# A two-layer hybrid block on one core: the experts' later tokens fetched by indirect DMA, their outputs added from a table in DRAM

## The chip, the core and the metric

The kernel runs on one core of a Trainium2 chip. A core has five engines with a queue of instructions each: TensorE (PE in the profile; its weight loads are PEld) multiplies matrices into PSUM banks, VectorE (DVE) and ScalarE (ACT) work on tiles in SBUF and PSUM, GpSimd (POOL) and SyncE (SP) here issue transfers, which 16 DMA engines carry out. Engines wait for each other by semaphores. The metric is the time of one execution on the device in microseconds; lower is better.

## What is computed

The input is 256 latent tokens and 256 context tokens of width 1024, all in float32, batch 1. An even layer (spatial gating beside windowed attention, then a dense SwiGLU) is followed by an odd layer (a recurrent block, then a mixture of experts) and a final RMSNorm. The change lies in the experts:

```python
def swiglu(t, w1, w3, w2):
    return (jax.nn.silu(t @ w1) * (t @ w3)) @ w2

def moe_swiglu(h, router_w, w1, w3, w2):
    logits = (t @ router_w).astype(jnp.float32)
    top_v, top_i = lax.top_k(logits, TOP_K)              # 2 of 8 experts
    gk = jax.nn.softmax(top_v, axis=-1)
    gates = jnp.sum(jax.nn.one_hot(top_i, N_EXPERTS) * gk[..., None], axis=1)
    for e in range(N_EXPERTS):
        out = out + gates[:, e:e + 1] * swiglu(t, w1[e], w3[e], w2[e])

    x = x + g2 * moe_swiglu(rmsnorm(x, n2) * (1.0 + sc2) + sh2, router_w, w1, w3, w2)
```

Per expert w1 and w3 are 1024 x 2816 and w2 is 2816 x 1024, so the eight experts' weights are 277 MB. Each token uses two experts, 64 tokens per expert on average.

## The kernel before

**Three products for one.** A float32 product is formed as three TensorE products of two-part numbers (`mm3`, L335 to L338): each operand is a high part, rounded to TensorE's 32-bit format, and a low part, the rest. So every half of a weight tile (128 x 1024 numbers, half of a raw tile of 1 MB) is split: ScalarE casts the high part `wh` (L126), VectorE subtracts it to get the low part `wl` (L127).

**The weight stream.** The class `Stream` has the list of all weight tiles in the order of their use (`units`). `pump_dma` issues a tile's load on the SP queue (L112) as soon as a raw buffer is free; there are twelve of them in the expert stage. `pump` issues the splits as soon as a pair of split buffers is free; there are five pairs (`HA`, `HB`). `get` hands a half to the matmuls, and what was put off with `later(n, f)` is issued n calls of `get` later.

**Experts.** Up to 128 tokens per expert are gathered into 128 slots. A dispatch matrix of zeros and ones (`make_disp`, `put_disp`, L1325) has a row per token and a column per slot. For a pair of experts `gather` multiplies the normalised rows (high and low part, `h2H`, `h2L`, tile hH) by the pair's 256 columns, 32 matmuls of 256 columns (L1381); this gives the rows already turned, features in partitions. ScalarE applies scale and shift (L1399) and casts (L1404), VectorE subtracts (L1405), into `xTH` and `xTL` (tile hLa).

An expert's 2816 inner columns are worked in six steps (`steps`, widths `GW`, five of 512 and one of 256). In each, `moe_p` forms t @ w1 and t @ w3 in one PSUM bank each (tag mm, four banks); ScalarE applies Silu (L1432), VectorE multiplies (L1434) into `s1`; `moe_t` turns it with TensorE transposes (L1441), and ScalarE and VectorE split it into `mg` (L1448, L1451); `moe_o` multiplies by w2 into two banks per expert (tag po). The loop over k issues `moe_p` of step k, then `moe_o` of step k-1, then `moe_t` of step k. Weight rows of w1 and w3 are 2 KB in a tile of four blocks of 128 rows (1 KB in the last step), those of w2 4 KB.

After an expert's last step `moe_y` multiplies the output by the layer's gate (L1485) and splits it (L1486, L1487). `combine` brings it back to tokens: the dispatch matrix, turned (`turn_disp`, L1414), times the output, 4 x 2 matmuls of 512 columns (L1495, L1496), and VectorE adds each of the four results, times the router's gate, to the residual `Xl` (L1498). Should an expert have over 128 tokens, `overflow` repeats it for the rest at the end.

**Order.** The functions are called in the order of the program, but a scheduler places each instruction on its engine's queue by its own reckoning of when its inputs are there; `issue_after` forces an order between two. Within a queue the order is fixed.

Of the kernel before, what the change touches and what calls it, by code (L numbers as in the profile page):

```python
# [14 lines left out]
I32 = mybir.dt.int32  # L15
# [196 lines left out]
def tile_block(ctx, tc, a, out):  # L212
# [3 lines left out]
    GW = [512] * 5 + [256]  # L216
# [37 lines left out]
    def moe_p_units(e, g, w1, w3):  # L254
        r = []
        for nm, w in (("m1", w1), ("m3", w3)):
            if GW[g] == 512:
                r += [kunit((nm, e, g, u), w, 4 * u, 4, 512 * g, 512) for u in range(2)]
            else:
                r.append(kunit((nm, e, g, 0), w, 0, 8, 512 * g, 256))  # L260
        return r

    def moe_o_units(e, g, w2):
        return [kunit(("m2", e, g, u), w2, 4 * g + 2 * u, 2, 0, D) for u in range(GW[g] // 256)]
# [32 lines left out]
    steps = [(e, g) for e in range(NE) for g in range(6)]  # L297
# [9 lines left out]
    NRAW, NRAW_X, NRAW_B = 4, 1, 7 - 1  # L307
# [366 lines left out]
    with ExitStack():  # L674
# [643 lines left out]
        yt, mg, n_t = [], [], [0]  # L1318
# [16 lines left out]
        def route_rest():  # L1335

            d = moe.tile([P, 4, 2], F32, name="dr")
            V.tensor_tensor(d[:, 0], mx[:, :, 1], mx[:, :, 0], op=ALU.subtract)
# [29 lines left out]
        xT, yo, gTs, yHL, dTs = {}, {}, {}, {}, {}  # L1368

        def gather(dst_key, dsp, n):  # L1370

            tH = moe.tile([P, KT, 256], F32R, tag="xTH", name=nm("xTH"))
            tL = xTL
            done = []
            terms = [(h2H, 0), (h2L, 0), (h2H, 1), (h2L, 1)]

            def add(p, c2, x):
                h, i = terms[x]
                for j in range(2):
                    cs = slice(P * (2 * c2 + j), P * (2 * c2 + j) + P)  # L1380
                    T.matmul(p[:, 256 * j:256 * j + n], h[:, i, cs], dsp(i), start=(x == 0 and j == 0), stop=(x == 3 and j == 1))  # L1381
            if dst_key == 0:
                ps = [mm() if c2 < 2 else po() for c2 in range(KT // 2)]
                for x in range(3):
                    for c2 in range(KT // 2):
                        add(ps[c2], c2, x)
            for c2 in range(KT // 2):
                if dst_key == 0:
                    p = ps[c2]
                    add(p, c2, 3)  # L1390
                else:
                    p = tr()
                    for x in range(4):
                        add(p, c2, x)
                js = slice(2 * c2, 2 * c2 + 2)
                tm = ht().rearrange("p (j f) -> p j f", j=2)[:, :, :n]
                for j in range(2):
                    c = 2 * c2 + j
                    x = S.activation(tm[:, j], p[:, 256 * j:256 * j + n], AF.Identity,  # L1399
                                     scale=AB[:, 1, 0, 0, c:c + 1], bias=AB[:, 1, 0, 1, c:c + 1])  # L1400
                if dst_key == 0:
                    V.tensor_copy(tH[:, js, :n], tm)  # L1402
                else:
                    S.copy(tH[:, js, :n], tm)  # L1404
                y = V.tensor_tensor(tL[:, js, :n], tm, tH[:, js, :n].bitcast(F32), op=ALU.subtract)  # L1405
                done.append((x, y))
            xT[dst_key] = tH, tL
            return done
# [9 lines left out]
        def moe_p(s_, e, g, x, c0):  # L1418
            xh, xl = x
            w = GW[g]  # L1420
            p1, p3 = mm(), mm()
            nk = 1024 // w
            s1 = ht()
            for name, p in (("m1", p1), ("m3", p3)):
                for u in range(8 // nk):
                    wH, wL = views(s_.get((name, e, g, u // 2)), nk)
                    for k in range(nk):
# [231 lines left out]
```

## Time and profile before

| | us |
|---|---|
| median of three runs (1600.59 to 1602.11) | 1601.19 |
| the profiled execution's own time | 1600.52 |
| its span, first to last instruction | 1598.7 |
| TensorE busy | 1551.5 |
| VectorE busy | 1286.8 |
| ScalarE busy | 981.1 |
| GpSimd busy | 0.2 |

The expert stage runs from about 808 us, where its first matmul starts, to 1582 us. What follows is the last expert's combine, the final norm and the stores. Busy time says how much an engine had to do, not whether the others waited for it: that is read from the waits and from the chain of work that ended last. TensorE's matmuls overlap in the records, so the cost of one on the path is the distance between the starts of two.

### The profile page before, as it was taken

How to read it: one execution, taken by the hardware profiler on the slowest of the kernel's cores; microseconds unless marked ns; L12 is line 12 of the kernel's file. 1: busy time of each engine (PE TensorE's matmuls, PEld its weight loads, DVE VectorE, ACT ScalarE, POOL GpSimd, SP SyncE). 2: the span in 40 equal slices, each digit the busy share in tenths (PEclk: the TensorE clock that was granted, in tenths of full speed). 3: DMA queues.
4: the chain of work that ended last, by engine and by line, in shares of the span. 5: the costliest groups of instructions: out<-in, count | busy, mean ns of one | idle time of the engine just before them, and what ended most of it. 6: DMA issues, size and time to landing. Idle time of an engine off the chain costs nothing.

```text
span 1598.7 us, 20230 instructions
## 1 busy us (share of the span) xinstructions
PE 1551.5 (97%) x7518; PEld 1237.4 (77%) x7518; DVE 1286.8 (80%) x1817; ACT 981.1 (61%) x1292; POOL 0.2 (0%) x4
## 2 busy tenths in 40 slices
PE   5999999999999999999999999999999999999996
PEld 3775787888888887776578888888888888888885
DVE  3577557475877576599899998998989899898987
ACT  4435625322222224679688877887778777877775
POOL 0000000000000000000000000000000000000000
PEclk9999999999999999999999999999999999999998
DMA  8867143444536441414699989999999999999980
GB/s 296 284 220 241 49 134 106 158 134 156 193 124 211 156 142 57 132 53 164 213 358 352 378 325 370 322 380 354 363 363 330 369 364 367 336 346 367 365 303 29
DMA packets 204267, 398.22 MB, mean 249 GB/s; under 512 B 7930, under 2 KB 66552, under 8 KB 204160
## 3 DMA queue, kind: packets, MB, share of 16 engines
q1 hardware_dynamic: 201184, 395.34, 69.7%
q10 hardware_dynamic: 2976, 1.50, 0.4%
q8 instruction: 61, 1.00, 0.3%
q14 instruction: 46, 0.38, 0.1%
HBM read 395.76 MB, written 1.05 MB: 248 GB/s over the span
## 4 chain that ended last, share of the span: by engine, by line
PE 87%; DVE 8%; ACT 2%; DMA 2%; issue 1%; ACTq 0%; DVEq 0%
PE mm L337 18%; PE mm L336 18%; PE mm L338 18%; PE po L337 8%; PE po L338 8%; PE po L336 8%; PE po L430 1%; PE tr L1441 1%; DVE wl L127 1%; PE po L983 1%; PE tr L1381 1%; PE tr L968 1%; DVE xn L500 1%; DMA raw<-in_w_in_e_dram 1%; DMA raw<-in_ada_w_o_dram 1%
## 5 line engine op out<-in xcount | busy, mean ns | idle before, releaser
L126 ACT CAST wh<-raw 128x1024 fp32r<-128x1024 f32 (+1 forms) x644 | 662.5, 1046 | 447.0 <-PE mm L337 145.4
L127 DVE TENSOR_TENSOR wl<-raw,wh 128x1024 fp32r<-128x1024 f32 (+1 forms) x644 | 759.4, 1214 | 127.5 <-ACT wh L126 115.9
L338 PE MATMUL mm<-wh,hLa 128*128 128x512 f32 (+1 forms) x800 | 299.2, 374 | 0.1
L337 PE MATMUL mm<-wl,xTH 128*128 128x512 f32 (+1 forms) x768 | 289.9, 377 | 0.0
L336 PE MATMUL mm<-wh,xTH 128*128 128x512 f32 (+1 forms) x768 | 287.3, 374 | 0.9 <-DVE xTH L1402 0.9
L336 PE MATMUL mm<-hH,wh 128*128 128x512 f32 (+1 forms) x608 | 228.7, 378 | 1.7 <-ACT gT L1148 1.5
L338 PE MATMUL mm<-hH,wl 128*128 128x512 f32 (+1 forms) x608 | 224.8, 371 | 0.5 <-DVE wl L127 0.5
L338 PEld LDWEIGHTS mm<-wh,hLa 128*128 128x128 f32 x800 | 150.9, 189 | 26.4 <-DVE hLa L1405 1.3
L337 PEld LDWEIGHTS mm<-wl,xTH 128*128 128x128 f32 x768 | 144.8, 189 | 27.1 <-DVE wl L127 3.0
L336 PEld LDWEIGHTS mm<-wh,xTH 128*128 128x128 f32 x768 | 144.8, 188 | 26.5 <-DVE xTH L1402 1.5
L337 PE MATMUL po<-wl,mg 128*128 128x512 f32 x352 | 137.4, 390 | 0.0
L338 PE MATMUL po<-wh,mg 128*128 128x512 f32 x352 | 136.4, 390 | 0.0
L336 PEld LDWEIGHTS mm<-hH,wh 128*128 128x128 f32 x608 | 114.2, 189 | 24.0 <-issue 2.0
L338 PEld LDWEIGHTS mm<-hH,wl 128*128 128x128 f32 x608 | 114.5, 188 | 20.1 <-DVE wl L127 0.7
L336 PE MATMUL po<-wh,mg 128*128 128x512 f32 x352 | 128.9, 391 | 0.0
L337 PE MATMUL mm<-hLb,wh 128*128 128x512 f32 (+1 forms) x304 | 112.9, 372 | 0.6 <-DVE hLb L616 0.6
L337 PE MATMUL mm<-hLa,wh 128*128 128x512 f32 (+1 forms) x304 | 112.8, 371 | 0.5 <-DVE hLa L616 0.5
L500 DVE SCALAR_TENSOR_TENSOR xn<-raw,act,xn 128x512 f32<-128x512 f32 x112 | 81.7, 747 | 1.2
L337 PEld LDWEIGHTS po<-wl,mg 128*128 128x128 f32 x352 | 66.2, 188 | 13.8 <-DVE wl L127 0.4
L336 PEld LDWEIGHTS po<-wh,mg 128*128 128x128 f32 x352 | 66.2, 188 | 13.5
L338 PEld LDWEIGHTS po<-wh,mg 128*128 128x128 f32 x352 | 66.0, 188 | 13.5
L337 PE MATMUL po<-wl,gH 128*128 128x512 f32 x176 | 69.9, 397 | 0.0
(392 smaller groups left out, 1873.9 us busy)
## 6 DMA issues: line engine op xcount, KB each, us to landing
raw<-in_moe_w_dram SPq DMA_DIRECT2D x264, 1024.0 KB
raw<-in_ffn_w_dram SPq DMA_DIRECT2D x33, 1024.0 KB
raw<-in_ada_w_e_dram SPq DMA_DIRECT2D x24, 1024.0 KB
raw<-in_ada_w_o_dram SPq DMA_DIRECT2D x24, 1024.0 KB
raw<-in_w_in_o_dram SPq DMA_DIRECT2D x10, 1024.0 KB
raw<-in_w_in_e_dram SPq DMA_DIRECT2D x7, 1024.0 KB
raw<-in_w_out_o_dram SPq DMA_DIRECT2D x5, 1024.0 KB
raw<-in_w_out_e_dram SPq DMA_DIRECT2D x2, 1024.0 KB
```

The costliest lines, as they stand in the source:

```text
L126: sp = (self.nc.scalar.copy(hv, src), self.nc.vector.tensor_tensor(lv, src, hv.bitcast(F32), op=ALU.subtract))
L127: self.nc.vector.tensor_tensor(lv, src, hv.bitcast(F32), op=ALU.subtract))
L336: T.matmul(dst, aH, bH, start=start, stop=False)
L337: T.matmul(dst, aH, bL, start=False, stop=False)
L338: return T.matmul(dst, aL, bH, start=False, stop=stop)
L430: T.matmul(p[32 * g:32 * g + 32, :], act[:, 4 * u + g, :], w[:, g, :], start=(u == 0), stop=(u == 1))
L500: V.scalar_tensor_tensor(acc[s_], w[:, k, :], c, acc[s_], op0=ALU.mult, op1=ALU.add)
L968: T.transpose(p[:, P * b:P * b + P], pr[:, P * b:P * b + P], ident)
L983: T.matmul(ob[c][0][64 * i:64 * i + 64, P * t:P * t + P], vv[:, b, 64 * i:64 * i + 64], pts[i][:, P * jj:P * jj + P], start=(jj == 0), sto ...
L1381: T.matmul(p[:, 256 * j:256 * j + n], h[:, i, cs], dsp(i), start=(x == 0 and j == 0), stop=(x == 3 and j == 1))
L1441: T.transpose(p[:, P * j:P * j + P], s1[:, P * j:P * j + P], ident)
```

## The change

**Weights.** The inner columns are worked in three steps of 1024, 1024 and 768. A raw tile of w1 or w3 has two blocks of 128 rows with 4 KB (3 KB in the last step) per row; a half is one block. `moe_p` now fills two banks for w1 and then two for w3; `s1` is a tile of its own of 1024 columns with one buffer (tag s1), and `mg` has one buffer instead of two halves. The raw buffers in the stage are eleven instead of twelve.

**Later tokens.** Only the first pair is gathered by matmuls (`gather_first`). GpSimd forms the normalised rows (`tokens`, in two halves, in the buffer with tag s1) and stores them in a table `Hd` in DRAM. `places` computes, for each token and choice, the slot (`put`) and the row of the output table (`take`); four indirect DMAs write the token's number into the slot's place in `Td`, which is read back as `slots`. `rows_of` fetches a later pair's rows from `Hd` by these numbers, during the even expert before, and `turn_slots` turns them with 16 transposes; scale, shift and split follow as before (`modulated`).

**Outputs.** `moe_y` of experts 0 to 6 stores the gated output in a table `Yd`; neither the split nor `combine` is done for them. `combine_table` fetches for each token and choice the row of `Yd` (a row of zeros where the choice is expert 7 or the token is in the overflow), and `add_table` adds it, times the router's weight, to the residual. Expert 7 goes the old way.

The diff, cut to its core:

```diff
-    GW = [512] * 5 + [256]
+    GW = [1024, 1024, 768]
+    NG = len(GW)
...
     def moe_p_units(e, g, w1, w3):
...
+        return [kunit((nm, e, g, u), w, 2 * u, 2, 1024 * g, GW[g], cut)
+                for nm, w in (("m1", w1), ("m3", w3)) for u in range(KT // 2)]
...
-    NRAW, NRAW_X, NRAW_B = 4, 1, 7 - 1
+    NRAW, NRAW_X, NRAW_B = 4, 1, 5
...
+        def rows_of(idx):
+
+            r = big("hH", [P, len(idx), D], F32)
+            for x, ids in enumerate(idx):
+                nc.gpsimd.indirect_dma_start(r[:, x, :], None, Hd[:, :], bass.IndirectOffsetOnAxis(ap=ids, axis=0))
+            return r
+
+        def turn_slots(keys, r):
+
+            tH = x_tile()
+            for c2 in range(KT // 2):
+                p = tr()
                 for j in range(2):
...
+                    for x in range(len(keys)):
+                        c = P * (2 * c2 + j)
+                        T.transpose(p[:, 256 * j + P * x:256 * j + P * x + P], r[:, x, c:c + P], ident)
+                modulated(tH, c2, p, P * len(keys), S.copy)
...
         def moe_p(s_, e, g, x, c0):
+
             xh, xl = x
...
+            cols = [slice(c, min(c + 512, GW[g])) for c in range(0, GW[g], 512)]
+            s1 = moe.tile([P, D], F32, tag="s1", name=nm("s1"))
+            for name in ("m1", "m3"):
+                ps = [mm() for _ in cols]
+                for k in range(KT):
+                    wH, wL = s_.get((name, e, g, k // 2))
+                    for p, cs in zip(ps, cols):
+                        mm3(p[:, :cs.stop - cs.start], xh[:, k, c0:c0 + P], xl[:, k, c0:c0 + P], wH[:, cs], wL[:, cs],
+                            k == 0, k == KT - 1)
...
         def moe_y(e):
...
+            if e in range(NE - 1):
+                y = big("hLb", [P, D], F32)
+                for h in range(2):
+                    cs = slice(512 * h, 512 * h + 512)
+                    V.tensor_tensor(y[:, cs], yo[e][h], gates["ao", 5, 0][:, cs], op=ALU.mult)
+                nc.gpsimd.dma_start(Yd[P * e:P * e + P, :], y)
+                return
...
+        def places():
...
+            for c in range(2):
+                for i in range(2):
+                    nc.gpsimd.indirect_dma_start(Td[:, :], bass.IndirectOffsetOnAxis(ap=put[:, c, i:i + 1], axis=0),
+                                                 toki[:, i:i + 1], None, bounds_check=NE * P - 1, oob_is_err=False)
+            nc.gpsimd.dma_start(slots_of, Td.rearrange("(e p) o -> p (e o)", p=P))
...
+        def add_table(r):
+            for c in range(2):
+                for i in range(2):
+                    V.scalar_tensor_tensor(Xl[:, i, :], r[:, 2 * c + i, :], g12[0][:, 2 + c, i:i + 1], Xl[:, i, :],
+                                           op0=ALU.mult, op1=ALU.add)
...
+        def tokens():
+
+            nc.gpsimd.memset(zero, 0)
+            nc.gpsimd.dma_start(Td.rearrange("(e p) o -> p (e o)", p=P), zero)
...
+            z = moe.tile([P, D], F32, tag="s1", name="zrow")
+            nc.gpsimd.memset(z[0:1, :], 0.0)
+            nc.gpsimd.dma_start(Yd[(NE - 1) * P:, :], z[0:1, :])
+            for t in range(2):
+                r = moe.tile([P, D], F32, tag="s1", name=nm("hrow"))
+                nc.gpsimd.tensor_scalar(r, Xl[:, t, :], rr[t], None, op0=ALU.mult)
+                nc.gpsimd.dma_start(Hd[P * t:P * t + P, :], r)
...
-        done = gather_pair(0)
+        done = gather_first()
+        tokens()
...
+                if e % 2 == 0 and g == 2 and e + 2 < NE:
+                    table[:] = [rows_of([slots_of[:, x:x + 1] for x in (e + 2, e + 3)])]
+                if e % 2 == 1 and g == NG - 1 and e + 1 < NE:
+                    turn_slots((e + 1, e + 2), table.pop())
+            if k >= 2 and steps[k - 2] == (NE - 1, NG - 1):
+                combine(NE - 1, dTs.pop(NE - 1), lambda i: G[:, i, NE - 1:NE])
...
-            if k == 3:
+            if k == 1:
                 with tc.issue_after(st.last[0].ins), tc.issue_after(st.last[1].ins):
                     route_rest()
+                    places()
...
+                if steps[k - 1] == (NE - 2, NG - 1):
+                    table[:] = [combine_table()]
+                if steps[k - 1] == (NE - 1, 0):
+                    with tc.issue_after(st.last[1].ins):
+                        add_table(table.pop())
```

**On GpSimd**, which had nothing of this before, there now stands at the start of the expert stage (with the semaphores that a row waits for; the row ISA in between reloads the engine's library):

```order
L1582 MEMSET zero_6343 128x8 [waits DVE_49,PE_49,Activation_49]
L1589 MEMSET zrow_6491 1x1024
L1583 DMA Td_6342<-zero_6343 128x8x1 [waits Pool_49]
L1590 DMA Yd_6341<-zrow_6491 16x1x64 [waits Pool_49]
L1593 ISA
L1593 TENSOR_SCALAR hrow_808_6494<-Xl_73,n1r_790_6363 128x1024 [waits DMASW1_49,DVE_49]
L1594 DMA Hd_6340<-hrow_808_6494 128x1024 [waits Pool_49]
L1593 TENSOR_SCALAR hrow_809_6497<-Xl_73,n1r_796_6395 128x1024 [waits DMASW2_49,DVE_49]
L1594 DMA Hd_6340<-hrow_809_6497 128x1024 [waits Pool_49]
```

The zero row, the two table rows and the first product tile share one buffer, so each row waits for the store of the one before it. What waits for the last of these stores (DMASW3) is ScalarE's first Silu of the experts, here in ScalarE's queue of the changed kernel among the weight casts:

```order
L126 CAST wh1171_6589<-raw117_6324 128x1024 [waits DVE_49,PE_49]
L126 CAST wh1180_6601<-raw118_6326 128x1024 [waits DMAHW5_49,DVE_49,PE_49]
L1453 ACT_TABLE_LOAD [waits DMASW2_49,DMASW3_49,DMASW1_49]
L1453 ACTIVATE s1_810_6514<-mm_811_6515 128x512 [waits Pool_49]
L126 CAST wh1181_6612<-raw118_6326 128x1024 [waits DVE_49,PE_49]
```

Before, the first Silu waited for its matmuls alone. wh1120 is the first half tile of the experts, so wh1180 is the thirteenth; the first product needs the first eight.

**On TensorE**, at the turn from experts 0 and 1 to 2 and 3, there stood before the gather of the next pair (tr) among the matmuls of the step before (po):

```order
L1381 MATMUL tr_8149<-disp_8019,hH_6338 128x256 x8
L1381 MATMUL tr_8163<-disp_8019,hH_6338 128x256 x8
L336 MATMUL po_7580<-wh_8077,mg 128x512
L1381 MATMUL tr_8177<-disp_8019,hH_6338 128x256 x8
L337 MATMUL po_7580<-wl_8078,mg 128x512
```

and now there stand the transposes of the fetched rows:

```order
L1425 MATMUL tr_8108<-ident,hH_7261 128x128 x4
L1425 MATMUL tr_8118<-ident,hH_7261 128x128 x4
L335 MATMUL po_7818<-wh_8063,mg 128x512
L336 MATMUL po_7818<-wl_8064,mg 128x512
L337 MATMUL po_7818<-wh_8063,mg 128x512
L335 MATMUL po_7819<-wh_8063,mg 128x512
L336 MATMUL po_7819<-wl_8064,mg 128x512
L1425 MATMUL tr_8128<-ident,hH_7261 128x128 x4
```

The 32 gather matmuls of the pair have become 16 transposes, the last four of them four matmuls further down.

**On VectorE**, at the handover into the experts, between the first weight split and the last part of x, the dispatch rows for expert 7 (and its neighbour) have moved up; now there stands:

```order
L127 TENSOR_TENSOR wl_6423<-raw_6176,wh_6422 128x1024
L1324 TENSOR_SCALAR disp_12162<-CT,pos,M 128x128 x2
L1382 CAST xTH_6428<-ht_6459 128x512
L1324 TENSOR_SCALAR disp_12162<-CT,pos,M 128x128
L1383 TENSOR_TENSOR hLa_6337<-ht_6459,xTH_6428 128x512
L1382 CAST xTH_6428<-ht_6466 128x512
L1324 TENSOR_SCALAR disp_12162<-CT,pos,M 128x128
```

Before, the same places followed each other without the rows of L1324 (there L1325). At the end, in the third step of expert 7, the four additions from the table stand in one block:

```order
L127 TENSOR_TENSOR wl3781_13101<-raw378_12845,wh3781_13100 128x768
L1570 SCALAR_TENSOR_TENSOR Xl_73<-hH_1015_12813,dr_6889,Xl_73 128x1024 x4
L127 TENSOR_TENSOR wl3790_13130<-raw379_12871,wh3790_13129 128x768
L127 TENSOR_TENSOR wl3791_13140<-raw379_12871,wh3791_13139 128x768
L1479 TENSOR_TENSOR mg_6693<-tr_1027_13116,mg_6693 128x512
```

Before, four additions of half rows followed each expert's combine.

## Rows read from the trace of the kernel before

**Rows 1.** Page, the span and part 1: busy us, share of the span, instructions

```profile
span 1598.7 us, 20230 instructions
...
PE 1551.5 (97%) x7518; PEld 1237.4 (77%) x7518; DVE 1286.8 (80%) x1817; ACT 981.1 (61%) x1292; POOL 0.2 (0%) x4
```

**Rows 2.** Stretch: its us, each engine's busy us, clock, DMA share, GB/s

```profile
820.00:1560.00 740.00, 740.00 (x3545) 617.83 (x3545) 688.12 (x746) 587.87 (x659) 0.00 (x0) 1.00 0.97 352
```

**Rows 3.** Waits, 820 to 1580 us: total us, times, longest

```profile
ACT wh L126 <- PE mm L338: 65.1, 165, 0.9
...
ACT wh L126 <- DMA raw<-in_moe_w_dram: 7.0, 21, 0.8
```

**Rows 4.** Waits of the SP queue, 820 to 1560 us

```profile
SPq L112 <- DVE wl L127: 565.6, 228, 5.5
```

**Rows 5.** Chain of waits, 850 to 1582 us: shares; start, us, what

```profile
by line: PE mm L337 20.7%; PE mm L336 20.5%; PE mm L338 20.5%; PE po L338 10.7%; PE po L337 10.7%; PE po L336 10.7%; PE tr L1441 2.5%; PE tr L1381 1.6%; PE tr L1496 0.9%; PE tr L1495 0.9%; PE tr L1414 0.2%; PE po L1349 0.0%
...
990.52 1.92 PE tr L1381 x16
```

**Rows 6.** Chain of waits, 1573 to 1600 us

```profile
1573.10 0.12 PE mm L338
...
1574.51 0.46 PE po L338 x2
...
1577.69 0.22 PE tr L1441 x2
```

**Rows 7.** Groups of instructions, 850 to 1582 us, shapes apart

```profile
L1381 PE MATMUL tr<-disp,hH 128*128 128x256 f32 x96 | 13.4, 285 | 0.0
...
L1495 PE MATMUL tr<-hLb,dispT 128*128 128x512 f32 x28 | 11.0, 393 | 0.0
...
L1414 PE MATMUL tr<-ident,disp 128*128 128x128 f32 x16 | 3.1, 273 | 0.0
...
L1498 DVE SCALAR_TENSOR_TENSOR Xl<-tr,G,Xl 128x512 f32<-128x512 f32 x28 | 20.4, 745 | 0.8 <-PE tr L1496 0.8
...
L1487 DVE TENSOR_TENSOR hLb<-ht,hLb 128x512 fp32r<-128x512 f32 x14 | 9.5, 684 | 0.0
L1486 ACT CAST hLb<-ht 128x512 fp32r<-128x512 f32 x15 | 9.1, 620 | 6.0 <-DVE ht L1485 5.6
...
L1399 ACT ACTIVATE ht<-tr,AB 128x256 f32<-128x256 f32 x24 | 12.3, 563 | 4.4 <-PE tr L1381 2.7 <-DVE hLa L1405 1.7
```

**Rows 8.** VectorE in order of time, 786 to 850 us: start, us

```profile
795.98 0.69 DVE L660 TENSOR_TENSOR Xl<-Xl,rtmp 128x512 f32<-128x512 f32 x1
...
801.73 0.60 DVE L1325 TENSOR_SCALAR disp<-CT,pos,M 128x128 fp32r<-128x128 f32 x2
...
803.20 1.28 DVE L1531 SCALAR_TENSOR_TENSOR hH<-Xl,n1r,hH 128x1024 fp32r<-128x1024 f32 x1
...
808.11 0.43 DVE L1402 CAST xTH<-ht 128x512 fp32r<-128x512 f32 x1 [0.58 <-ACT ht L1399]
...
814.51 9.29 DVE L127 TENSOR_TENSOR wl<-raw,wh 128x1024 fp32r<-128x1024 f32 x8
```

**Rows 9.** DMA, 820 to 1560 us: packets, issues of weight tiles

```profile
DMA packets 117547, 260.65 MB, mean 352 GB/s; under 512 B 3984, under 2 KB 20368, under 8 KB 117498
...
raw<-in_moe_w_dram SPq DMA_DIRECT2D x246, 1024.0 KB
```

**Rows 10.** Two stretches of 3 us: 2 KB rows, then 4 KB

```profile
874.00:877.00 3.00, 3.00 (x15) 2.48 (x14) 3.00 (x4) 2.74 (x4) 0.00 (x0) 1.00 1.06 408
1205.50:1208.50 3.00, 3.00 (x15) 2.47 (x14) 3.00 (x4) 2.63 (x4) 0.00 (x0) 1.00 1.01 416
```

**Rows 11.** ScalarE in order of time, 786 to 850 us

```profile
799.39 2.19 ACT L1517 ACTIVATE hH<-Xl,n1r 128x1024 fp32r<-128x1024 f32 x2 [0.15 <-DVE n1r L542]
...
808.86 1.05 ACT L126 CAST wh<-raw 128x1024 fp32r<-128x1024 f32 x1
```

**Rows 12.** VectorE in order of time, 1578 to 1600 us

```profile
1590.15 1.42 DVE L1630 SCALAR_TENSOR_TENSOR xn<-Xl,n1r,fn 128x512 f32<-128x512 f32 x2
```

More of the change, by code (lines that the diff above doesn't have):

```diff
@@ L296, in tile_block @@
     n_dense = len(units)
-    steps = [(e, g) for e in range(NE) for g in range(6)]
+    steps = [(e, g) for e in range(NE) for g in range(NG)]
     for k in range(len(steps) + 1):
@@ L1407, in gather @@
-            xT[dst_key] = tH, tL
-            return done
+                    T.matmul(p[:, 256 * j:256 * j + 256], h[:, i, cs], d[:, i, :], start=(x == 0 and j == 0),
+                             stop=(x == 3 and j == 1))
+            ps = [mm() if c2 < 2 else po() for c2 in range(KT // 2)]
+            for x in range(3):
+                for c2 in range(KT // 2):
+                    add(ps[c2], c2, x)
+            done = []
+            for c2 in range(KT // 2):
+                add(ps[c2], c2, 3)
+                done.append(modulated(tH, c2, ps[c2], 256, V.tensor_copy))
@@ new lines, in moe_t, with evac @@
+            for c in range(0, GW[g], 512):
+                w = min(512, GW[g] - c)
+                p = tr()
+                for j in range(w // P):
+                    T.transpose(p[:, P * j:P * j + P], s1[:, c + P * j:c + P * j + P], ident)
+                def evac(p=p, cs=slice(c, c + w), w=w):
+                    with tc.issue_after(S.copy(gH[:, cs], p[:, :w]).ins):
+                        if last and cs.stop == GW[g]:
+                            S.activation(small.tile([P, 1], F32, tag="warm", name="warm2"), CT[:, C_ONE:C_ONE + 1],
+                                         AF.Sqrt)
+                    V.tensor_tensor(gL[:, cs], p[:, :w], gH[:, cs].bitcast(F32), op=ALU.subtract)
+                if last:
+                    evac()
+                else:
+                    s_.later(2 + c // 512, evac)
@@ L1465, in prod @@
                 return mm3(yo[e][h], gH[:, js], gL[:, js], w[0][:, cs], w[1][:, cs],
-                           g == 0 and k == 0, g == 5 and k == 1)
-            if key == steps[-1]:
-                w = s_.get(("m2", e, g, 0), n=2)
-                for h in range(2):
-                    for k in range(2):
-                        last = prod(k, h, w[k])
-                return last
-            for k in range(GW[g] // P):
+                           g == 0 and k == 0, g == NG - 1 and k == n - 1)
+            end = 2 if key == steps[-1] else 0
+            for k in range(n - end):
                 w = s_.get(("m2", e, g, k // 2))
```

189 lines of the change are left out of this document (97 added, 92 removed).

## The prediction

> **What bounds the kernel now.** I read the page first: the TensorE row is busy for 97% of the span, VectorE for 80%, ScalarE for 61%, GpSimd for nothing (four memsets) [rows 1]. Busy shares are averages over stages, so next came the table of stretches: from 820 to 1560 us, the expert stage, TensorE has no idle time at all, VectorE is at 93% (688 of 740), ScalarE at 79%, the granted clock is 1.00 (the 2.4 GHz level) and the DMA engines have work for 97% of the time [rows 2]. Three engines near their ends: the waits tell which one leads. ScalarE's splitting casts wait for TensorE to give back a split buffer (65.1 us in the first matrices alone), but only 7.0 us in all, in 21 waits of at most 0.8 us, for a weight tile to land [rows 3]. The SP queue, which loads the weights, stood 565.6 of these 740 us waiting for VectorE to finish a raw tile, that is for space [rows 4]. So the weights run ahead, limited by buffers, the splits run ahead, limited by buffers, and what gives buffers back is TensorE. The chain of waits agrees: between 850 and 1582 us all of it is matmuls [rows 5]. A microsecond of TensorE work taken from this stage should be a microsecond of the time, as long as the second (VectorE) and third (DMA) do not become the first.
>
> What one piece costs on that path is read from the distances in the chain, not from the mean durations (0.39 us, which overlap): a 512-column matmul is 0.23 us (two in 0.46), a 256-column one 0.12, a 128x128 transpose 0.11 (two in 0.22) [rows 6].
>
> **The change part by part, on TensorE.** Removed: the gathers of the later three pairs of experts, 3 x 32 = 96 matmuls of 256 columns [rows 7], 16 of them in 1.92 us [rows 5], so 0.12 each and 11.5 us (the chain's 1.6% of 732 us is 11.7). The combine matmuls of experts 0 to 6, 28 of L1495 [rows 7] and as many of L1496, of 512 columns: 56 x 0.23 = 12.9 us (the chain: 1.8% of 732, 13.2). The transposes of the dispatch matrix of seven experts, 14 of the 16 [rows 7]: 14 x 0.11 = 1.5 us. Together 25.9 us. Added: 16 transposes for each of three pairs, 48 x 0.11 = 5.3 us. The sum on TensorE is -20.6 us. The weights' matmuls keep their number and shapes: per expert 48 of 256 columns and the rest of 512, only in another order, and the 22 transposes of the product per expert stay.
>
> **VectorE and ScalarE**, the cover of all this, get lighter. VectorE loses 28 additions into the residual (20.4 us) and 14 subtractions of L1487 (9.5), gains four whole-row additions; the row of that kind and size took 1.28 us (L1531 [rows 8]), so 5.1. ScalarE loses 14 of the 15 casts of L1486 (9.1 us) [rows 7]. The splits grow from 66 to 70 per expert, 16 of them of 768 columns. A full one takes 1.16 us back to back (eight in 9.29 [rows 8]); one of 768 lies between three quarters of that, 0.87, and the whole, and I take 0.9. TensorE uses it up in 3 x 0.23 + 3 x 0.12 = 1.05 us. So VectorE stays the follower in the third group of an expert too, and I cost the new shapes at nothing; that cover is gone if a 768-column split takes over 1.05 us.
>
> **The weight rows of 4 KB** change no wait that is on the path: DMA is ahead now. What they must do is carry the added traffic: 1 MB to the table of rows, 3 MB gathered, 3.5 MB of outputs written, 2 MB read back. Beside weights at TensorE's shorter pace that asks (260.65 MB of before [rows 9] and 9.5 x 1.05 = 10 MB) over 720 us = 376 GB/s, where 352 flowed [rows 2]; there are 3 us stretches at 408 GB/s, of 2 KB rows, and at 416, of 4 KB rows [rows 10]. I cost it at nothing, and the opposite is a rival below. One raw buffer fewer of twelve makes the lead of the loads shorter by a twelfth; with 7 us of waiting for loads in the whole stage that is free as well.
>
> **What stands in the way of the whole 20.6 us.** (a) Handover: four dispatch rows of VectorE (0.60 us for two [rows 8]) now stand between the first weight split and the last tile of x, where TensorE waits for VectorE. Two fall into the 0.58 us that VectorE idles there, two do not: +0.6. (b) At each pair's turn TensorE does 8 transposes, five matmuls, 4 transposes, four matmuls, 4 transposes. The third and fourth group wait for ScalarE to empty a bank (two rows of 0.563 us [rows 7], with casts of 1.05 between [rows 11]). Before, the matmuls of a group took 0.96 us (half of the 1.92), now 0.44, so there is less cover. From nothing (if ScalarE is on time) to about 2 us a pair (two banks, a cast each); I take 0.6, so +1.8 for three. (c) The four additions from the table stand in VectorE's queue as one block of 5.1 us, in the last expert's third group, with five split buffers of 1.05 us = 5.2 us ahead of it: 0 to 2 us, I take 0.5. If the table's rows are not there yet, this block waits with all later splits queued behind it. From the last output's product to the block there are 24 splits, some 31 us at TensorE's pace, for 0.5 MB written and 2 MB gathered; at 352 GB/s that is 7 us. (d) GpSimd's chain at the start, with no row of its kind before. The first product tile s1 shares one buffer with the zero row and both table rows, so the first Silu waits until the second store has landed, and ScalarE's casts queue behind it. The chain starts when the residual is done, 796.7 us (L660 at 795.98 + 0.69 [rows 8]): a memset, a store, a multiply, a store, a multiply, a store. Its lower end: two multiplies at 1.1 us (ScalarE did such rows at 2.19 for two [rows 11]) and two half MB at 416 GB/s, 5 us, so 802. An upper end from the farthest rows: three computing steps at 1.28 and three stores at the 7.1 us that lie between VectorE's last row (1590.15 + 1.42) and the end of the span [rows 12, 1], 25 us, so 822. The Silu is due once the eighth half tile of the step is used: its split ends at about 819.2 (the fourth of eight after 814.51), so 820.5; by then five more halves are split, 5 x 6 x 0.23 = 6.9 us, and TensorE starves only from 827.4. By both ends the cost is nothing, and I take 0; the library reload in front of the multiply has no price in any row, and neither has the making of 1024 four-byte pieces for the first store, so this is where the largest error can come from.
>
> The Trainium skill, GPSIMD Engine Reference, section 2.1 Instruction dispatch, says that the first call of a freshly loaded kernel on GpSimd pays about 6 us more. No run here shows it yet; with it the upper end would be 828, an estimate, and the sum half a microsecond smaller.
>
> **The sum:** -20.6 + 0.6 + 1.8 + 0.5 = -17.7 us. The profiled execution took 1600.52 us (its span of 1598.7 and 1.8 around it), so 1582.8; it was 0.7 below the median of 1601.19, to which the prediction is put: 1583.5 us. The end of the program (expert 7's combine and the final norm, 1582 to 1598.7) is unchanged.
>
> **Rivals.** First, late on GpSimd, the one that ends slower: the reload and the piecewise first store take so long that the second table row lands after 827.4. Each further microsecond holds ScalarE, then VectorE, then TensorE, one for one. Landed at 845 the gain is gone, from 848 on the time is slower than before; at 860 the time is 1583.5 + 33 = 1616. For it: seven steps in one queue of which no row has a price. Against it: it needs over 18 us more than the upper end above. Second, the DMA becomes the bound: if 352 GB/s is all that the stream sustains, 270.65 MB take 769 us in place of 740, +29. The loads' lead, by my estimate eight of the twelve raw tiles landed and waiting, 3.0 us each (740 us for 246 tiles [rows 9]), is eaten up first, 24, so 5 us stay: about 1606. For it: DMA engines at 97%. Against it: the SP queue's 565.6 us of waiting for space, and the 408 and 416 GB/s.
>
> The Trainium skill speaks for that rival: DMA: Bandwidth & Descriptors, section Where 436 GB/s comes from, has about 358 GB/s as what HBM gives one core. The trace does not agree with it as a ceiling here, with 416 GB/s in a stretch; taken as one, the stage's bytes would need 756 us, +16 less the lead of 24, and the time would be about 1593, that of the third rival, with which it shares its chance.
>
> Third, nothing dramatic but more small change: the turns of (b) at 2 us, the block of (c) at 2, some of (d): -20.6 + 0.6 + 6 + 2 + 3, so about 1592.
>
> **How the numbers follow.** My forecast 0.70, its own range 1579 to 1589. Late GpSimd 0.15: 0.08 of it still faster, 0.03 about the same, 0.04 slower. DMA-bound 0.06, slower. More small change 0.09, all faster. A difference under 0.2% (3.2 us) is what a measurement of this kernel cannot tell from no change. Faster: 0.70 + 0.08 + 0.09 = 0.87, of which I move 0.03 to the same, for a mix of the small costs and the chain; same 0.06; slower 0.04 + 0.06 = 0.10. The range has to reach into the late chain: 1577 to 1598.
>
> **What would show it.** Right: matmuls in the chain from about 810 to 1561 without a gap, no gather matmuls for the later pairs but 48 transposes; ScalarE's waits for TensorE, not for DMA; the second table store landed before 827. Wrong: a hole of TensorE near 825 to 840 with the first Silu waiting (rival one); casts waiting for weight tiles by tens of us and a stretch at 352 GB/s (rival two); VectorE waiting for the table's rows near 1545 (part c); holes of over 1 us at the three pair turns (part b).

## The result, and the profile after

The changed kernel took 1610.8 us (median of 4 runs, 1608.9 to 1611.6) beside 1600.9 us before (4 runs, 1599.9 to 1602.1): a ratio of 1.0054, interval 1.0041 to 1.0066. It is slower by 10 us, where 17.7 us less were forecast. The profiled execution:

```profile
span 1608.8 us, 20156 instructions
...
PE 1545.7 (96%) x7400; PEld 1223.6 (76%) x7400; DVE 1272.5 (79%) x1819; ACT 978.6 (61%) x1303; POOL 49.5 (3%) x34
```

TensorE, VectorE and ScalarE all have less work than in [rows 1], and yet the span is longer. The expert stage as one stretch, to be read against [rows 2]: TensorE was busy for all of its 740 us before, and now is not for 16.3 of them.

```profile
820.00:1560.00 740.00, 723.72 (x3393) 594.23 (x3392) 663.73 (x729) 579.40 (x663) 39.20 (x26) 0.99 0.97 365
```

Cut into shorter stretches (busy us of PE, PEld, DVE, ACT, POOL, then the clock, DMA share, GB/s), most of it is in one place:

```profile
830.00:842.00 12.00, 0.33 (x2) 0.10 (x1) 0.12 (x1) 2.96 (x4) 3.68 (x3) 0.72 0.22 91
842.00:849.00 7.00, 6.53 (x15) 4.77 (x16) 6.79 (x6) 5.80 (x7) 0.00 (x0) 0.51 0.70 239
849.00:880.00 31.00, 31.00 (x140) 25.05 (x139) 28.76 (x57) 25.07 (x28) 0.00 (x0) 1.00 0.76 252
```

For 12 us TensorE and VectorE do next to nothing, ScalarE little (2.96 us), and the weight transfers stop; for the next 7 us the granted clock is 0.51, the 1.2 GHz level. What they wait for is read backwards, engine by engine. TensorE in order of time (start, us; in brackets its idle time and what ended it):

```profile
829.84 0.40 PE L337 MATMUL mm<-wh,hLa 128*128 128x512 f32 x1
841.90 0.79 PE L335 MATMUL mm<-wh,xTH 128*128 128x512 f32 x1 [11.67 <-ACT wh L126]
843.16 0.79 PE L336 MATMUL mm<-wl,xTH 128*128 128x512 f32 x1 [0.47 <-DVE wl L127]
843.75 0.63 PE L337 MATMUL mm<-wh,hLa 128*128 128x512 f32 x1
844.18 0.63 PE L335 MATMUL mm<-wh,xTH 128*128 128x512 f32 x1
```

It waited for a cast of ScalarE. ScalarE had stood for 14.7 us at the first Silu:

```profile
823.27 1.05 ACT L126 CAST wh<-raw 128x1024 fp32r<-128x1024 f32 x1 [0.34 <-DMA raw<-in_moe_w_dram]
839.03 1.28 ACT L1453 ACT_TABLE_LOAD   x1 [14.71 <-DMA Hd<-hrow]
```

The Silu waited for the second store of scaled rows, since its tile s1 shares a buffer with them. And GpSimd, which makes and stores these rows:

```profile
797.77 1.08 POOL L1583 DMA_DIRECT2D Td<-zero  x1
798.85 0.56 POOL L1590 DMA_DIRECT2D Yd<-zrow  x1
812.48 16.84 POOL L1593 TENSOR_SCALAR hrow<-Xl,n1r 128x1024 f32<-128x1024 f32 x1 [13.07 <-DMA Yd<-zrow]
829.61 0.63 POOL L1594 DMA_DIRECT2D Hd<-hrow  x1 [0.30 <-POOL hrow L1593]
832.84 2.84 POOL L1593 TENSOR_SCALAR hrow<-Xl,n1r 128x1024 f32<-128x1024 f32 x1 [2.60 <-DMA Hd<-hrow]
835.98 0.59 POOL L1594 DMA_DIRECT2D Hd<-hrow  x1 [0.30 <-POOL hrow L1593]
```

Two things in it are long: 13 us until the 4 KB zero row has landed, behind the 1024 four-byte pieces of Td, and 16.84 us for the first multiply against 2.84 for the second of the same shape. VectorE in that time:

```profile
815.16 11.43 DVE L127 TENSOR_TENSOR wl<-raw,wh 128x1024 fp32r<-128x1024 f32 x10
841.88 1.22 DVE L127 TENSOR_TENSOR wl<-raw,wh 128x1024 fp32r<-128x1024 f32 x1 [15.29 <-ACT wh L126]
```

Ten subtractions back to back end at 826.59; the multiply ends at 829.32, 2.7 us later: as if it had only run once VectorE was idle.

**The second loss has no hole.** The hole and the slow clock are worth about 15 us (11.8 between the two starts beyond one matmul, and 3.4 in the 7 us at half clock). Against the forecast 28 are missing (1610.9 us for the profiled execution, 1582.8 forecast for it). The other waits of the stage are small. ScalarE's, 820 to 1560 us (total, times, longest), for [rows 3]:

```profile
ACT wh L126 <- PE mm L337: 84.7, 213, 1.2
...
ACT L1453 <- DMA Hd<-hrow: 14.7, 1, 14.7
ACT ht L1380 <- PE tr L1425: 5.1, 2, 2.5
...
ACT wh L126 <- DMA raw<-in_moe_w_dram: 1.7, 5, 0.4
```

Weights are not late (1.7 us, 7.0 before). So the distances between matmuls have to be read, to more digits than the prediction did. TensorE in order of time in the third expert, first the kernel before, then the changed one; from the second matmul of a product to the first of the next, without a wait in between:

```profile
1050.07 0.39 PE L337 MATMUL mm<-wl,xTH 128*128 128x512 f32 x1
...
1060.75 0.39 PE L336 MATMUL po<-wh,mg 128*128 128x512 f32 x1
```

```profile
1009.57 0.40 PE L336 MATMUL mm<-wl,xTH 128*128 128x512 f32 x1
...
1031.74 0.39 PE L335 MATMUL po<-wh,mg 128*128 128x512 f32 x1
```

Before, 47 matmuls in 10.68 us, 227 ns each; now 95 in 22.17, 233 ns. Over the whole stage (820 to 1560 us) the mean distance from a 512-column matmul with xTH or hLa to the next is 228.0 ns before and 233.3 now (distances over 300 ns left out, which are waits or missing records); "spacing" below is this mean. Both round to 0.23. There are 5 x 2 x 8 x 3 x 8 = 1920 of them (512-column groups, matrices, blocks of rows, products, experts): 10 us. Near the end the same trace has both speeds within one kind of product, with the stationary operand in mg, and then in mgl, which is the buffer of xTH:

```profile
1580.15 0.39 PE L337 MATMUL po<-wh,mg 128*128 128x512 f32 x1
...
1584.23 0.40 PE L337 MATMUL po<-wh,mg 128*128 128x512 f32 x1
...
1586.33 0.39 PE L336 MATMUL po<-wl,mgl 128*128 128x512 f32 x1
...
1592.63 0.39 PE L337 MATMUL po<-wh,mgl 128*128 128x512 f32 x1
```

18 steps in 4.08 us, 227 ns, against 27 in 6.30, 233 ns. What sets mgl and xTH apart is their place. In the built program the seven small tiles that the change declares (zero, put, take, slots, two for tokens, lts; 32 bytes each) lie ahead of xTH and move it from byte 162,432 of its partition, a multiple of 128, to 162,656, which leaves 96. mg, ahead of them, stays at a multiple of 128 (152,192), and hLa belongs to a pool that is laid out earlier. These addresses come from the program; no trace shows them. The matmuls with hLa are late with the others: from a matmul with hLa to the next one with xTH it is 227.6 ns before and 232.7 now, from one with xTH to the one with hLa 228.0 and 232.7, between the two with xTH 228.3 and 234.6.

### The profile page after: what moved, and what is told of

It reads as the page before. It is cut to its first block, busy times and chain, and to the rows that moved or that the text cites. A ratio compares the mean times of both kernels' runs of the same rounds, so it can differ in the third digit from the quotient of the medians.

```text
span 1608.8 us, 20156 instructions
## 1 busy us (share of the span) xinstructions
PE 1545.7 (96%) x7400; PEld 1223.6 (76%) x7400; DVE 1272.5 (79%) x1819; ACT 978.6 (61%) x1303; POOL 49.5 (3%) x34
## 5 line engine op out<-in xcount | busy, mean ns | idle before, releaser
L126 ACT CAST wh<-raw 128x1024 fp32r<-128x1024 f32 (+2 forms) x676 | 671.6, 1006 | 460.9 <-PE mm L336 144.8
L127 DVE TENSOR_TENSOR wl<-raw,wh 128x1024 fp32r<-128x1024 f32 (+2 forms) x676 | 766.4, 1163 | 156.8 <-ACT wh L126 148.4
L335 PE MATMUL mm<-wh,xTH 128*128 128x512 f32 (+1 forms) x768 | 272.8, 381 | 13.3 <-ACT wh L126 12.3
L336 PE MATMUL po<-wl,mg 128*128 128x512 f32 x340 | 133.2, 392 | 1.9 <-DVE wl L127 1.9
L337 PE MATMUL po<-wh,mg 128*128 128x512 f32 x340 | 132.9, 391 | 0.0
L335 PE MATMUL po<-wh,mg 128*128 128x512 f32 x340 | 114.8, 392 | 1.6 <-ACT wh L126 1.6
L335 PEld LDWEIGHTS po<-wh,mg 128*128 128x128 f32 x340 | 63.3, 188 | 15.3 <-ACT wh L126 2.5
L337 PEld LDWEIGHTS po<-wh,mg 128*128 128x128 f32 x340 | 63.8, 188 | 13.0
```

The lines of the kernel that those rows point to most:

```text
L126: sp = (self.nc.scalar.copy(hv, src), self.nc.vector.tensor_tensor(lv, src, hv.bitcast(F32), op=ALU.subtract))
L127: self.nc.vector.tensor_tensor(lv, src, hv.bitcast(F32), op=ALU.subtract))
L335: T.matmul(dst, aH, bH, start=start, stop=False)
L336: T.matmul(dst, aH, bL, start=False, stop=False)
L337: return T.matmul(dst, aL, bH, start=False, stop=stop)
```

## The experiments

There are two theories for the two losses, each with a rival. The Silu's wait for the row store is on the path (or something else would have been late anyway). The address of xTH costs the 5 to 6 ns a matmul (or the two banks that now alternate every three matmuls do).

**align.** The address alone:

```
+        pad = moe.tile([P, 8], F32, name="pad")
         zero = moe.tile([P, 8], I32, name="zero")
```

Expected: 

> One unused tile of 32 bytes per partition is put ahead of the experts' small tiles, so that xTH (the transposed tokens, stationary operand of the m1 and m3 products) begins at byte 162,688 of its partition, a multiple of 128, and no longer at 162,656, which leaves 96. Nothing else changes. Theory A (the address of xTH): the 1920 matmuls of 512 columns with xTH or hLa go from a mean of 233.3 ns apart back to 227.3, so 11.5 us leave: 1610.8 - 11.5 = about 1599. Rival B (two mm banks that alternate every three matmuls cost the 6 ns): spacing stays at 233.3 and the time at 1611. Rival C (the matmuls are not what sets the pace, something else is late): spacing falls, time does not, 1608 to 1611.

Measured: 1595.7 us (12 runs, 1593.0 to 1601.1), ratio 0.9971 [0.9959, 0.9982] to before; spacing 227.9 ns. In the third expert:

```profile
1007.42 0.39 PE L336 MATMUL mm<-wl,xTH 128*128 128x512 f32 x1
...
1028.98 0.39 PE L335 MATMUL po<-wh,mg 128*128 128x512 f32 x1
```

95 in 21.56 us, 227 ns: 32 unused bytes brought the old pace back, as theory A has it. The hole is still there in its profile (11.9 us of idle time), and the profiled execution (span 1599.2, 9.6 under the changed kernel's) was the slowest of the twelve. The median is 15.1 us under the changed kernel, more than the address accounts for; what the faster runs saved besides, a shorter hole perhaps, no trace shows.

**serp.** The rival's own test, no address changed:

```
-                    for p, cs in zip(ps, cols):
+                    for p, cs in list(zip(ps, cols))[::1 - 2 * (k % 2)]:
```

Expected: 

> In moe_p the two banks of a product are taken in the order 0,1 for even k and 1,0 for odd k, so the bank changes after every six matmuls and no longer after every three. Addresses are as in the changed kernel. Theory A (the address of xTH): spacing of the 512-column matmuls stays at 233 ns, 1611 us. Rival B (a change of bank costs some 18 ns, spread over three matmuls): half of the changes go, spacing about 230 ns, 1611 - 5.8 = about 1605.

Measured: 1609.4 us, ratio 1.0044 [1.0029, 1.0059], spacing 233.1 ns. Half of the bank changes are gone and the spacing has not moved, so rival B falls.

**mis32** does to the kernel before what the change did by accident:

```
+        pad = moe.tile([P, 8], F32, name="pad")
         d0 = moe.tile([P, 2, 256], F32R, tag="disp", name="disp0")
```

Expected: 

> The kernel before, with one unused tile of 32 bytes per partition ahead of disp0, which moves xTH from byte 162,432 (a multiple of 128) to 162,464 (32 over one). Theory A (the address of xTH): the 1920 matmuls of 512 columns with xTH or hLa go from 227.3 to about 233 ns apart, 1600.9 + 11 = about 1612. Rival B (alternating banks): no bank alternates in these products here, spacing stays at 227 and the time at 1601.

Measured: 1607.8 us, ratio 1.0040 [1.0028, 1.0053], spacing 232.1 ns. The loss follows the address into a kernel without table, alternating banks or 4 KB rows. Its size (6.5 us) is under the 11 expected, since the spacing grew by 4 ns and not by 6.

**mis64x** moves xTH by 64 bytes in the kernel before, with one pad between disp and xTH and one behind xTH:

```
+        pad1 = moe.tile([P, 16], F32, name="pad1")
...
+        pad2 = moe.tile([P, 16], F32, name="pad2")
```

Expected: 

> The kernel before with 64 unused bytes per partition ahead of xTH and 64 more behind it: xTH begins at byte 162,496, which is 64 past a multiple of 128, and every tile behind it is moved by 128. Theory A1 (what counts is a multiple of 64): the 512-column matmuls with xTH or hLa stay 227 ns apart, 1601 us. Theory A2 (what counts is a multiple of 128): about 232 ns, as with the shift by 32, 1608 us.

Measured: 1610.2 us in one run, spacing 232.6 ns, as theory A2 has it. Here xTH alone left its multiple of 128, since all that lies behind it moved by 128. Offsets of 32, 64 and 96 past a multiple of 128 were all slow, 0 was fast.

**hrow.** The rows leave the buffer of s1:

```
+            rows = big("hH", [P, 2, D], F32)
             for t in range(2):
-                r = moe.tile([P, D], F32, tag="s1", name=nm("hrow"))
+                r = rows[:, t, :]
```

Expected: 

> GpSimd writes the two blocks of scaled rows for the token table into hH (free once the first gather's matmuls are done) and no longer into the buffer of s1, so the first Silu does not wait until the second block has landed. GpSimd's own chain stays as long as it is. Theory A (that wait is the hole of TensorE from 829.8 to 841.9, and the slow clock behind it is part of its price): 11.7 us of idle time and 14 matmuls at 0.43 us apart instead of 0.233 (2.8 us) leave, 1610.8 - 14.5 = about 1596, with no idle time of TensorE over 2 us between 812 and 860. Rival B (the weight transfers, which stood still from 830 to 845, would have been late anyway): a new wait of the casts for raw tiles takes its place, 1603 to 1611.

Measured: 1595.7 us (1594.0 to 1596.4), ratio 0.9963 [0.9951, 0.9976]; TensorE runs through 829.8 to 841.9 without a gap. That is 15.2 us less than the changed kernel, where 14.5 were expected: the hole was on the path, and nothing took its place.

**both** (the edits of align and hrow). Expected: 

> The edits of align (32 unused bytes per partition, xTH at a multiple of 128 bytes) and of hrow (GpSimd's scaled rows in hH) together. Theory (two costs that have nothing to do with each other: the wait at the start, and 6 ns on each of 1920 matmuls): the time of hrow, 1595.7, less the 9.6 us by which the profiled span of align stood under that of the changed kernel (1608.8 to 1599.2) = about 1586, between 1584 and 1588; spacing 227 ns, no idle time of TensorE over 2 us between 812 and 860. Rival (the weight transfers become the bound once TensorE is that fast): the casts wait for raw tiles, 1590 or more.

Measured: 1586.5 us (1585.2 to 1586.9), ratio 0.9900 [0.9884, 0.9915], spacing 227.9 ns. The pad takes 9.2 us from hrow's time, which agrees with the 9.6 between the two profiled spans and the 10 of the spacing. The medians alone do not add up: align and hrow took 15.1 and 15.2 us one by one, and 24.3 together; the 6 us between are what align's faster runs saved beyond the address. With both losses gone the change is faster than the kernel before, so nothing else made it slower.

**rowsonly.** Half of the change: the groups of 1024, 1024 and 768 columns and five B buffers in the kernel before; gathers and combines as in before:

```
-    GW = [512] * 5 + [256]
+    GW = [1024, 1024, 768]
...
-    NRAW, NRAW_X, NRAW_B = 4, 1, 7 - 1
+    NRAW, NRAW_X, NRAW_B = 4, 1, 5
```

Expected: 

> The kernel before with one half of the change: weight rows of 4 KB (groups of 1024, 1024 and 768 columns, s1 as one tile, five B buffers, moe_p, moe_t and moe_o of the changed kernel). Tokens of later experts still come by one-hot matmuls, outputs are still combined by matmuls after each expert; there is no table. xTH stays at 162,432. Theory A (the prediction's zero for the rows: the transfers had slack, TensorE has the same work): 1599 to 1603. Rival B (larger rows themselves are a gain): under 1598. Rival C (fewer buffers, a longer last group cost): 1604 or more.

Measured: 1602.5 us, ratio 1.0002 [0.9992, 1.0011], as theory A has it. The rows are worth nothing either way; the gain of both is the table's. The banks alternate here too, with xTH at its old address, and the spacing is 228.2 ns: against rival B once more.

**Why was GpSimd so late?** Three runs on its chain. **warm** pays any first-use price early:

```
+    nc.gpsimd.memset(lg, 0.0)
+    nc.gpsimd.tensor_scalar(lg, lg, 1.0, None, op0=ALU.mult)
```

Expected: 

> The changed kernel with two small GpSimd instructions more at the very start of the program: a memset of lg (128x16) and a tensor_scalar on it. Nothing else changes; the rows still go through the buffer of s1, xTH still begins 96 bytes past a multiple of 128. Theory A (the first tensor_scalar of 16.84 us at 812.5, against 2.84 us for the second, holds some 14 us in which GpSimd fetches the code for it): that is now paid at the start, the rows at 812.5 take 2.8 us, the second block lands at about 825, before the first Silu is due at 827, and the hole goes: about 1596. Rival B (the first one is slow because of what else runs at 812 to 829: VectorE's subtractions or the transfers): it stays at 17 us and the time at 1611.

Measured: 1609.0 us (12 runs, 1601.6 to 1615.3), ratio 1.0038 [1.0026, 1.0051]. GpSimd in order of time:

```profile
0.94 0.26 POOL L389 TENSOR_SCALAR lg<-lg 128x16 f32<-128x16 f32 x1
...
816.13 17.27 POOL L1595 TENSOR_SCALAR hrow<-Xl,n1r 128x1024 f32<-128x1024 f32 x1 [12.67 <-DMA Yd<-zrow]
```

The instruction had been used at 0.94 us, behind the library reload, and at 816 it is as long as in the changed kernel. Theory A of this run fell; its rival B stands, that the instruction is slow because of what else runs there.

**gpmem** keeps place and size, but reads nothing; it leaves out the scaling, so its table of rows holds zeros:

```
-                nc.gpsimd.tensor_scalar(r, Xl[:, t, :], rr[t], None, op0=ALU.mult)
+                nc.gpsimd.memset(r, 0.0)
```

Expected: 

> The changed kernel with GpSimd's two multiplies (rows scaled into the buffer of s1) replaced by memsets of the same tiles; the scaling is left out, the table of rows holds zeros. Buffers, stores and order stay. Theory L (the first multiply did not run for 14 of its 16.84 us because it reads SBUF while VectorE's subtractions with two SBUF inputs stand back to back up to 826.6): a memset reads nothing, takes 1 to 2 us at 812.5, the second block lands by 822, before the first Silu is due at 827, and the hole goes: about 1596. Rival B (any GpSimd instruction has to wait there until VectorE is idle): the first memset ends at about 828, the second block lands at about 836, most of the hole stays, about 1608.

Measured: 1599.1 us (1595.9 to 1601.3), ratio 0.9987 [0.9978, 0.9997]. GpSimd, then VectorE:

```profile
813.20 0.95 POOL L1593 MEMSET hrow<- 128x1024 f32 x1 [11.65 <-DMA Yd<-zrow]
814.45 0.58 POOL L1594 DMA_DIRECT2D Hd<-hrow  x1 [0.30 <-POOL hrow L1593]
822.32 0.95 POOL L1593 MEMSET hrow<- 128x1024 f32 x1 [7.29 <-DMA Hd<-hrow]
```

```profile
815.88 11.43 DVE L127 TENSOR_TENSOR wl<-raw,wh 128x1024 fp32r<-128x1024 f32 x10
```

The second memset takes 0.95 us in the middle of the same ten subtractions, so rival B falls: what is held off there is the multiply, which reads, and not the memset. The time is 3 us over the 1596 expected: each store of rows now took over 7 us to land, so the second was late for 827 after all, and a hole of 2.7 us stayed. Why a store is slower there was not tried. In the changed kernel, where GpSimd waited 2.6 us for it, the subtractions were over, but the weight transfers had all but stopped too.

**tdlast** issues the 1024 pieces behind the rows:

```
-            nc.gpsimd.dma_start(Td.rearrange("(e p) o -> p (e o)", p=P), zero)
...
+            with tc.issue_after(put_r.ins):
+                nc.gpsimd.dma_start(Td.rearrange("(e p) o -> p (e o)", p=P), zero)
```

Expected: 

> The changed kernel with the store of 1024 four-byte zeros (Td) issued behind the two stores of rows and no longer ahead of the zero row's store (Yd). Theory T (the zero row's 4 KB took 13.4 us only because the 1024 pieces went ahead of it on the same queue): it lands within 3 us of its issue, near 802, the first multiply starts there, where VectorE's instructions are of mixed kinds with gaps, and both blocks have landed by 820: no hole, 1596 to 1599. Rival (a store from GpSimd takes 13 us there whatever stands ahead): the multiply starts at 811 to 813 as before, 1609 to 1611.

Measured: 1602.8 us, ratio 1.0016 [1.0007, 1.0026]. It is a miss, above the 1596 to 1599 of its theory, and it tells the most. GpSimd, then VectorE:

```profile
803.34 3.63 POOL L1592 TENSOR_SCALAR hrow<-Xl,n1r 128x1024 f32<-128x1024 f32 x1 [4.79 <-DMA Yd<-zrow]
...
811.60 16.52 POOL L1592 TENSOR_SCALAR hrow<-Xl,n1r 128x1024 f32<-128x1024 f32 x1 [3.68 <-DMA Hd<-hrow]
```

```profile
813.97 11.43 DVE L127 TENSOR_TENSOR wl<-raw,wh 128x1024 fp32r<-128x1024 f32 x10
```

The zero row landed after 4.8 us in place of 13, so the pieces did hold the queue up. The first multiply then ran among VectorE's mixed short operations in 3.63 us. Now it is the second that meets the ten subtractions, and the second that lasts 16.5 us: it ends at 828.12, 2.7 us after they end at 825.40. Being first has nothing to do with it. A hole of 5.4 us stayed. The multiplies of hrow bear this out: they ran ahead of the subtractions, from 808.75 us, and took 5.90 us for both.

The Trainium skill, SBUF — State Buffer, section SBUF: two separate sides, says that VectorE and GpSimd share a pair of ports as an exclusive lock, and that a VectorE operation with two SBUF inputs takes it only against a GpSimd operation that reads SBUF. The three runs agree: 17.27 and 16.52 us for a multiply, 0.95 for a memset. The page has the loser wait for one instruction; measured, the multiply ended 2.7 us after the last of ten, as if it had not got in between them, and the measurement decides.

**late and best**, on top of both. late lets ScalarE make the rows after the first group's products; best also spreads the transposes of a pair's turn over the weight tiles of the product that runs there. late:

```
+        def scaled_rows():
+            rows = big("hH", [P, 2, D], F32)
...
+                r = rows[:, t, :]
+                S.activation(r, Xl[:, t, :], AF.Copy, scale=rr[t])
...
+            if k == 0:
+                with tc.issue_after(st.last[0].ins):
+                    scaled_rows()
```

and best has beside it:

```
-            for c2 in range(KT // 2):
+
+            def part(c2):
...
+                if len(keys) > 1:
+                    st.later((1, 2, 4, 6)[c2], lambda c2=c2: part(c2))
```

Expected: 

> The kernel of both edits (xTH at a multiple of 128 bytes, rows in hH), with the two blocks of rows made by ScalarE after the first group's products (some 2.2 us of ScalarE there) and no longer by GpSimd at 808.8 to 814.7. Theory (GpSimd's multiplies hold up VectorE's casts and one-input operations at the handover: 0.83 us for a cast in place of 0.42, 1.13 for a dispatch row in place of 0.34): TensorE's idle time of 2.03 us ahead of the first product falls back towards the 1.20 of the kernel before, and the time from 1586.5 to about 1585, between 1584 and 1586. Rival (ScalarE's 2.2 us show instead, since TensorE has few split buffers ahead there): 1587 to 1589.

Expected: 

> As late, and at the turns of the second to fourth pair the four groups of transposes with their activations are put in one at a time behind the first, second, fourth and sixth weight tile of the product that runs there, not all at once ahead of it. Theory (at two of the three turns ScalarE stands 2.57 us waiting for transposes that TensorE has not come to, its casts queue behind, and TensorE then loses 1.21 + 0.93 + 0.81 us in place of 3 x 0.23, so 2.3 us a turn): some 4 us less than late, about 1581, between 1580 and 1583. Rival (the last tile of x is now late for the next product, and the stall only moves): within 1 us of late.

Measured: late 1583.9 us (1582.5 to 1584.4), ratio 0.9895 [0.9879, 0.9912]; best 1579.2 us (1578.8 to 1580.2), ratio 0.9867 [0.9850, 0.9883]. Both theories held, each with a gain a little above the expected one. The wait that best removes, of ScalarE for a turn's transposes (the run both, 1165 to 1190 us), and then the expert stage of best as a stretch, with 0.7 us of TensorE idle in place of 16.3:

```profile
ACT ht L1380 <- PE tr L1425: 2.6, 1, 2.6
```

```profile
820.00:1560.00 740.00, 739.26 (x3545) 619.07 (x3544) 690.75 (x760) 604.24 (x691) 28.01 (x24) 1.00 0.97 368
```

best beats both kernels, the one before by 21.6 us and the changed one by 31.6.

## Why the prediction was wrong, point by point

- **The bound and the work on TensorE, -20.6 us: right.** With the two losses removed (the run both) the time is 14.4 us below before; with the small stalls of (a) and (b) removed as well (the run best), 21.6 below.
- **"The weights' matmuls keep their number and shapes": this step failed.** They do, and each was taken to cost what it had. 0.23 us, read from [rows 6] to two digits, hid a change of 227 to 233 ns: 10 us by the means, 9.2 between hrow and both. What failed is the price of a term taken as unchanged: tiles that a change only declares had no term in the sum, and they moved xTH.
- **(d), the GpSimd chain at nothing: this step failed.** Its upper end of 822 was put together from VectorE's and the end's rows; the second store landed at 839.0. Each of the three stores was taken at up to 7.1 us, and the zero row took 13.4 with the pieces ahead of it; a multiply was taken at up to 1.28 and the first took 16.84, the second 2.84. The prediction called the reload and the pieces its largest possible error. The pieces were about half of the 17 us (8.3 us by tdlast). The reload was not the rest (warm has it at the start and is as slow); that was the multiply that met VectorE's subtractions. It is rival 1 as it was described (a hole at 825 to 840, the first Silu waiting, each microsecond past 827.4 one for one): 11.6 us late gave a hole of 11.7. What that rival did not have is the slow clock behind the hole, 3 us more. By rival 1 alone, at 839, the time would have been about 1595; it took both losses together to end above before. The distance that spoke against this rival, "over 18 us" from the upper end to where the gain is gone, is 23 by the prediction's own figures (822 to 845).
- The sentence on GpSimd's first call (the Trainium skill, GPSIMD Engine Reference, section 2.1 Instruction dispatch) is not borne out by these runs: the first tensor_scalar of warm took 0.26 us.
- **4 KB rows and the added traffic at nothing: right** (rowsonly 1.0002; casts wait 1.7 us for weights in the changed kernel). Rival 2 is out: 369 GB/s flowed over the stage in the run both, and the casts waited for weights for 2.7 us in all.
- **768-column splits at nothing: right**; no wait of TensorE for them shows.
- **(a) handover, +0.6: too large.** TensorE, the kernel before and then the changed one:

```profile
806.54 0.65 PE L1381 MATMUL mm<-disp,hH 128*128 128x256 f32 x4
...
808.59 0.50 PE L336 MATMUL mm<-wh,xTH 128*128 128x512 f32 x1 [0.92 <-DVE xTH L1402]
```

```profile
806.53 1.05 PE L1397 MATMUL mm<-disp,hH 128*128 128x256 f32 x4
...
810.24 0.50 PE L335 MATMUL mm<-wh,xTH 128*128 128x512 f32 x1 [1.03 <-DVE xTH L1382]
```

  The idle time ahead of the first product grew by 0.1 us. The product starts 1.65 us later mostly because the gather ahead of it ran at a lower clock: 0.52 was granted from 806 to 808 us, and 1.00 before. This is not the change's doing: mis32, the kernel before with 32 unused bytes, has 0.50 from 804 to 806, and tdlast, with the whole change, 1.00.
- **(b) turns, +1.8: the size and the wait were wrong.** TensorE waits for a bank once, 0.5 us (in the run both). ScalarE stands in its own order at an activation whose transposes TensorE has not come to (2.5 us, twice), the casts queue behind, and TensorE pays 2.3 us at two of three turns (in the same run: 1.21 + 0.93 + 0.81 between starts in place of 3 x 0.23), 4.5 in all. best is 4.7 us faster than late, from which it differs by this alone.
- **(c) the additions, +0.5:** VectorE never waits for the table's rows; TensorE is idle for 0.6 us between 1520 and 1560.

## What to carry to other kernels

Before costing an edit, look at where it puts tiles: here seven small tiles ahead of a matmul's operand cost some 10 us, and a pad of 32 bytes gave it back. Read repeated instructions by start-to-start distance over a hundred of them, since a change of 3% did not show in two digits here. And do not let a chain on a new engine end in a buffer that the main path needs: here the length of that chain was set by what another engine happened to do then.

## What the hardware showed that was not expected

- 512-column fp32r matmuls with xTH or hLa start 228 ns apart when xTH lies at a multiple of 128 bytes in its partition (before, rowsonly, align, both), and 232 to 233 ns when it lies 32, 64 or 96 bytes past one (mis32, mis64x, the changed kernel). This was moved in both directions, in two kernels. Why is open.
- A GpSimd multiply of 128x1024 took 2.84 us beside an idle VectorE and 16.5 to 17.3 beside ten two-input subtractions back to back (changed kernel, warm, tdlast); a memset of that size took 0.95 there (gpmem).
- With a store of 1024 four-byte pieces ahead of it GpSimd waited 13 us for its 4 KB store, and 4.8 without (tdlast).
- After 12 us in which TensorE did next to nothing its granted clock was 0.51 for the next 7 us.
